# Decode forgetting attention in 32-column tiles of the array, with the cached values whole

## The chip, the core and the metric

One core of a Trainium2 chip runs the whole program in one launch. The metric is device time in microseconds. The kernel before took 3339.79 us (median of three runs, 3335.1 to 3340.51). Its profiled execution took 3333.96 us, of which 3331.8 us lie between the first and the last instruction.

## What is computed

The kernel is one step of a one-layer streaming encoder. A prompt of 2048 tokens and 8 decode streams of 16 new tokens each go through one input projection, three gated branches (forgetting attention, retention, attention into a memory) and an output projection. The change touches the forgetting attention, above all that of the decode streams, where 16 queries of a stream meet 2048 cached tokens and the 16 new ones, for 8 heads of 64:

```python
def fox_attend(q, c_q, q_pos, k, v, c_k):
    s = jnp.einsum('bqhd,bkhd->bhqk', q, k, preferred_element_type=jnp.float32) * (DH_FOX ** -0.5)
    s = s + jnp.swapaxes(c_q, 1, 2)[..., :, None] - jnp.swapaxes(c_k, 1, 2)[..., None, :]
    k_pos = jnp.arange(k.shape[1])
    s = jnp.where(k_pos[None, :] <= q_pos[:, None], s, -jnp.inf)
    p = jax.nn.softmax(s, axis=-1).astype(v.dtype)
    return jnp.einsum('bhqk,bkhd->bqhd', p, v)

# decode: the cache and the new tokens together
k_all = jnp.concatenate([cache_fox_k[l].astype(fk.dtype), fk], axis=1)
v_all = jnp.concatenate([cache_fox_v[l].astype(fv.dtype), fv], axis=1)
c_all = jnp.cumsum(jnp.concatenate([cache_fox_logf[l].astype(jnp.float32), logf], axis=1), axis=1)
fox_o = fox_attend(fq, c_all[:, past:], pos_s, k_all, v_all, c_all)
```

Everything is fp32. Most products are made in the type fp32r, a factor being split into a part that fp32r holds and the rest; some are plain fp32 matmuls.

## The kernel before

After the projection (to about 1690 us) two lanes are woven together by weights. The right lane runs retention and then the prompt's forgetting attention (`fox`: scores at L1290 to L1293, maxima L1297, exponentials L1298, factors by `softmax_scale`, scaling on GpSimd at L1302, transposes L1324, split L202 and L205, values L1344, end L1350 to L1352). The left lane runs a short scan, the prompt's memory attention, the decode memory attention and then `decode_fox`. When `decode_fox` is done the left lane begins the first output block beside the rest of `fox`, and then the other output blocks follow. All stages write their instructions in this woven order, and a scheduler then sets the order on each engine. All loads stand in SyncE's one queue (L184).

`decode_fox` does one `unit` per stream b, 8 of them, a new one entering every 5 steps, so that two or three are alive at once. A unit goes through its keys in four chunks of 512 cached tokens (ci = 0 to 3) and a last one of the 16 new tokens (ci = 4), first for the scores, then for the values.

- Rows of the score: 128 partitions hold 4 pairs of heads, 2 heads of a pair, 16 queries. A key tile `dkt` holds one pair of heads on its 128 partitions. The queries of pair g stand in `qb` as a 128x128 block that is zero but for the 32 columns of that pair (the tile is 160 wide and is read with a stride of 128, so that pair g falls on columns 32g to 32g+31). The four fp32 matmuls of a chunk (L1460) therefore each fill 128 rows, three quarters of them with zeros, and are added up in one bank `ys`; a matmul with 16 rows (L1461) adds the running sum of the forget logarithms from `crow`. `crow` is made at a unit's begin by 16 transposes (L1450) and four copies (L1451).
- L1469 takes the maximum of the chunk, L1471 the exponentials `dpt`. After the last chunk `softmax_scale` makes one factor per chunk: L1221 the smallest of the negated maxima `nmx`, L1222 a subtraction on VectorE, L1223 the exponential on ScalarE. GpSimd scales `dpt` (L1477).
- Values: four transposes (L1487) bring 512 tokens of `dpt` to PSUM, and L202 (ScalarE) and L205 (VectorE) split them into two halves of `dpr`, which stand side by side as 128 columns: 64 of the first part, 64 of the rest. Every 256 cached values `dvt` are split too, L1497 (ScalarE) making `dvh`, and L1499 (GpSimd, twice) the rest `dvl`. Four fp32r matmuls of 256 columns (L1504) for each block of 128 tokens then add into `ov`, tile `ym`. The last chunk uses the new values `dvn`, already split (L1511, L1512). L1514 copies `ov` (128x512), and four matmuls with `sumid` (L1520) add the two halves and transpose.

`softmax_scale` is also called by `fox`, with two blocks of queries (nq = 2).

Of the kernel before, what the change touches and what calls it, by code (L numbers as in the profile page):

```python
# [9 lines left out]
F32 = mybir.dt.float32  # L10
# [62 lines left out]
def body(ctx: ExitStack, tc: tile.TileContext, a, o, stop=99):  # L73
# [106 lines left out]
    def f32(t):  # L180
        return t.bitcast(F32)
# [1033 lines left out]
    def softmax_scale(nmx, l, f, nq, ncx, name):  # L1215

        if ncx == 1:
            V.reciprocal(f, l)
            return None
        nm = sp.tile([P, 2], F32, name=name + "nm")[:, :nq]  # L1220
        V.tensor_reduce(nm, nmx, AX.X, ALU.min)  # L1221
        V.tensor_tensor(f, nm.unsqueeze(2).broadcast_to([P, nq, ncx]), nmx, ALU.subtract)  # L1222
        S.activation(f, f, AF.Exp)  # L1223
        V.scalar_tensor_tensor(l, l, 2.0, f, ALU.mult, ALU.mult)
        V.tensor_reduce(nm, l, AX.X, ALU.add)
        V.reciprocal(nm, nm)  # L1226
        return nm
# [141 lines left out]
    def decode_fox(dp, dw):  # L1369
# [53 lines left out]
        qblk = [dp.tile([P, 4, 160], F32, name=f"qb{i}") for i in range(2)]  # L1423
# [3 lines left out]
        def unit(b):  # L1427

            z = qblk[b % 2]
            for hf in range(2):  # L1430
                rr = slice(64 * hf, 64 * hf + 64)
                G.tensor_copy(z[rr, :, hf * TS:(hf + 1) * TS], qw[rr, :, b * TS:(b + 1) * TS])
            qb = z.rearrange("p g c -> p (g c)")[:, :512].rearrange("p (g c) -> p g c", g=4)
# [18 lines left out]
            for ci in range(5):  # L1452
                sc = pys()
                if ci < 4:
                    w = 512
                    for g2 in range(2):
# [23 lines left out]
            for ci in range(5):  # L1480
# [4 lines left out]
                pr = dw.tile([P, 4, 2, 2, 64], F32R, name="dpr", bufs=1)  # L1485
                for j in range(n):
                    T.transpose(p[:rows, j * P:(j + 1) * P], pts[ci][:, j * P:j * P + rows], ident)  # L1487
                prv = pr.rearrange("p j a r c -> p (j a) r c")[:rows, :2 * n]
                split(prv[:, :, 0], prv[:, :, 1], p[:rows, :n * P].rearrange("p (a c) -> p a c", c=64))
                if ci < 4:  # L1490
                    for j in range(4):
                        if j % 2 == 0:
                            vt = dw.tile([P, 2, 512], F32, name="dvt")
                            dma(vt, vvw[:, 4 * ci + j:4 * ci + j + 2])
                            vh = dw.tile([P, 2, 512], F32R, name="dvh")
                            vl = dw.tile([P, 2, 512], F32R, name="dvl")
                            S.copy(vh, vt)  # L1497
                            for i in range(2):
                                G.tensor_tensor(vl[:, i], vt[:, i], f32(vh)[:, i], ALU.subtract)  # L1499
                        for part in (vh, vl):  # L1500
                            for a2 in range(2):
                                c = slice(a2 * 256, (a2 + 1) * 256)
                                lt = pr[:, j, a2].rearrange("p r c -> p (r c)")
                                T.matmul(ov[:, c], lt, part[:, j % 2, c], start=ci == 0 and j == 0 and a2 == 0 and part is vh, stop=False)  # L1504
                else:
                    vn = dw.tile([16, 8, P], F32R, name="dvn", bufs=1)
                    dma(f32(vn), f32(vhl)[SEQ + b * TS:SEQ + (b + 1) * TS])
                    for a2 in range(2):
                        c = slice(a2 * 256, (a2 + 1) * 256)
                        lt = pr[:16, 0, a2].rearrange("p r c -> p (r c)")  # L1510
                        T.matmul(ov[:, c], lt, vn[:, 4 * a2:4 * a2 + 4, 0:64], start=False, stop=False)  # L1511
                        T.matmul(ov[:, c], lt, vn[:, 4 * a2:4 * a2 + 4, 64:128], start=False, stop=a2 == 1)  # L1512
                    os = dw.tile([P, 512], F32, name="dos", bufs=1)
                    S.copy(os, ov)  # L1514
# [3 lines left out]
            for g4 in range(4):  # L1518
                c0 = 96 * g4 - 32 * (g4 % 2)
                T.matmul(p[:, c0:c0 + 64], os[:, g4 * P:(g4 + 1) * P], sumid, start=True, stop=True)  # L1520
            pv = p[:, :384].rearrange("p (g c) -> p g c", g=4)
# [273 lines left out]
```

## Time and profile before

| | |
|---|---|
| median of three runs | 3339.79 us |
| profiled execution | 3333.96 us |
| its span | 3331.8 us |
| mean granted TensorE clock | 0.978 |
| decode attention beside the prompt's, about 2004 to 2690 us | 686 us |
| TensorE busy in that stretch | 646.75 us |
| ScalarE, VectorE, GpSimd busy in it | 482.11, 480.04, 428.22 us |

TensorE's busy time is the union of its matmuls, and each of them is shown until its last result is out, while the next has begun already. What a matmul costs the engine is therefore read from the distance between two starts, and the `mean ns` of a group is longer than that. A plain fp32 matmul stands in the trace as two records, one behind the other; an fp32r matmul, or a transpose, as one. In the column of shapes, `128*128` is rows and columns of the array in use, and the shape behind it the moving tile. [...]

### The profile page before, as it was taken

To read this page: it belongs to the slowest core of one execution; us is meant where nothing else is said; L and a number is where in the kernel's file an instruction comes from. 1 tells how busy PE (TensorE), PEld (TensorE's weight loads), DVE (VectorE), ACT (ScalarE), POOL (GpSimd) and SP (SyncE) were. 2 spreads that over 40 slices of the span, in tenths; PEclk is the share of its full clock that TensorE was granted. 3 is DMA by queue.
4 is the path that set the end of the run, shared out by engine and by line. 5 is a ranking of instruction groups with operands and counts; after the bars stand their busy time and mean duration, and the time that the engine had idled before them with its cause. 6 is when DMAs were issued, how large, how long until landed. Compare 5 with 4: busy or idle time off the path is not lost.

```text
span 3331.8 us, 57569 instructions
## 1 busy us (share of the span) xinstructions
PE 3164.7 (95%) x21243; PEld 2900.8 (87%) x21243; DVE 2107.7 (63%) x3478; ACT 1655.8 (50%) x3217; POOL 981.8 (29%) x917
## 2 busy tenths in 40 slices
PE   6999999999999999999979978999999999999999
PEld 5999999999999999999969945777777788889899
DVE  7777676756556566556667736766666886554444
ACT  4453444545445455445445635767677774222222
POOL 4446443100210020210011303666665853100100
PEclk8999999999999999999989988999999999999999
DMA  4776565677556658767677875555565458576665
GB/s 165 234 241 210 186 199 192 197 221 238 184 175 202 203 185 244 225 201 212 199 246 236 271 224 174 156 157 163 176 200 156 121 155 252 178 214 198 183 201 160
DMA packets 638445, 660.75 MB, mean 198 GB/s; under 512 B 46060, under 2 KB 553348, under 8 KB 638100
## 3 DMA queue, kind: packets, MB, share of 16 engines
q1 hardware_dynamic: 638164, 657.08, 63.9%
q8 instruction: 168, 2.75, 0.3%
q14 instruction: 113, 0.93, 0.1%
HBM read 477.52 MB, written 179.41 MB: 197 GB/s over the span
## 4 chain that ended last, share of the span: by engine, by line
PE 69%; DMA 11%; DVE 9%; issue 4%; ACT 4%; POOL 2%; SPq 1%; DVEq 0%; ACTq 0%; POOLq 0%
PE a L449 7%; PE a L451 7%; PE a L450 7%; PE b L449 5%; PE b L451 5%; PE b L450 5%; PE ys L1460 3%; PE ov L1344 3%; PE tp L1324 3%; DMA x<-in_x_prompt 2%; DMA out_y_p<-x 2%; DVE wl L400 2%; PE sc L1290 2%; PE ym L1504 2%; PE tp L227 1%
## 5 line engine op out<-in xcount | busy, mean ns | idle before, releaser
L400 DVE TENSOR_TENSOR wl<-wr,wh 128x1024 fp32r<-128x1024 f32 (+1 forms) x386 | 565.1, 1468 | 287.0 <-ACT wh L399 285.1
L399 ACT CAST wh<-wr 128x1024 fp32r<-128x1024 f32 (+1 forms) x386 | 404.6, 1050 | 306.8 <-PE b L451 128.2
L449 PE MATMUL a<-wh,ho 128*128 128x256 f32 (+1 forms) x1432 | 407.3, 285 | 14.7 <-ACT gz L707 8.4
L450 PE MATMUL a<-wl,ho 128*128 128x256 f32 (+1 forms) x1432 | 405.5, 283 | 5.8 <-DVE wl L400 5.8
L451 PE MATMUL a<-wh,ho 128*128 128x256 f32 (+1 forms) x1432 | 406.1, 284 | 0.7 <-DVE ho L276 0.7
L451 PE MATMUL b<-wh,ho 128*128 128x256 f32 (+1 forms) x1032 | 290.8, 282 | 5.4 <-DVE ho L276 5.4
L449 PE MATMUL b<-wh,ho 128*128 128x256 f32 (+1 forms) x1032 | 291.4, 283 | 4.3 <-ACT wh L399 2.3
L450 PE MATMUL b<-wl,ho 128*128 128x256 f32 (+1 forms) x1032 | 290.7, 282 | 0.6 <-DVE wl L400 0.6
L449 PEld LDWEIGHTS a<-wh,ho 128*128 128x128 f32 x1432 | 272.4, 190 | 18.3 <-ACT gz L707 10.4
L221 ACT CAST wh<-wraw 128x1024 fp32r<-128x1024 f32 x120 | 122.9, 1049 | 331.0 <-DMA wraw<-in_w_p 121.7
L428 POOL TENSOR_TENSOR wr<-wr 128x1024 f32<-128x1024 f32 (+1 forms) x72 | 200.1, 2779 | 272.1 <-DMA wr<-in_w_in 219.7
L450 PEld LDWEIGHTS a<-wl,ho 128*128 128x128 f32 x1432 | 272.6, 190 | 6.3 <-DVE wl L400 6.3
L451 PEld LDWEIGHTS a<-wh,ho 128*128 128x128 f32 x1432 | 272.6, 190 | 1.3 <-DVE ho L276 1.3
L449 PE MATMUL a<-ho,wh 128*128 128x384 f32 (+1 forms) x768 | 253.0, 329 | 1.8 <-ACT gz L707 1.7
L450 PE MATMUL a<-ho,wh 128*128 128x384 f32 (+1 forms) x768 | 253.3, 330 | 0.0
L451 PE MATMUL a<-ho,wl 128*128 128x384 f32 (+1 forms) x768 | 252.6, 330 | 0.0
L460 ACT COPY kp<-a 128x256 f32<-128x256 f32 (+3 forms) x384 | 152.9, 404 | 183.3 <-PE a L451 182.7
L1297 DVE TENSOR_REDUCE f_mx<-sc 128x1 f32<-128x512 f32 (+2 forms) x320 | 192.2, 604 | 66.1 <-PE sc L1293 33.1
L1302 POOL TENSOR_SCALAR pt<-pt,f_f,f_nm 128x512 f32<-128x512 f32 (+3 forms) x288 | 206.0, 730 | 93.8 <-DVE f_nm L1226 78.7
L1298 ACT ACTIVATE pt<-sc,f_mx 128x512 f32<-128x512 f32 (+2 forms) x320 | 200.8, 628 | 63.5 <-DVE f_mx L1297 55.7
L205 DVE TENSOR_TENSOR pl<-tp,ph 128x512 fp32r<-128x512 f32 (+2 forms) x352 | 193.0, 562 | 55.8 <-ACT ph L202 52.9
L451 PEld LDWEIGHTS b<-wh,ho 128*128 128x128 f32 x1032 | 195.1, 189 | 5.6 <-DVE ho L276 5.6
(375 smaller groups left out, 8819.0 us busy)
## 6 DMA issues: line engine op xcount, KB each, us to landing
wr<-in_w_in SPq DMA_DIRECT2D x170, 512.0 KB
wraw<-in_w_p SPq DMA_DIRECT2D x80, 512.0 KB
dkt<-in_cache_fox_k SPq DMA_DIRECT2D x64, 512.0 KB
dvt<-in_cache_fox_v SPq DMA_DIRECT2D x64, 512.0 KB
wr<-sum_gl SPq DMA_DIRECT2D x48, 512.0 KB
wraw<-in_w_out SPq DMA_DIRECT2D x40, 512.0 KB
gtd<-gz SPq DMA_DIRECT2D x96, 192.0 KB
gt<-gtd SPq DMA_DIRECT2D x24, 768.0 KB
```

What stands on the lines that cost most here:

```text
L205: V.tensor_tensor(l, src, f32(h), ALU.subtract)
L221: S.copy(whv[:, i * hc:(i + 1) * hc], rv)
L399: S.copy(h, t)
L400: eng.tensor_tensor(l, t, f32(h), ALU.subtract)
L428: G.tensor_tensor(out, x, y, op)
L449: T.matmul(out, lh(c), rh(c), start=first and c == 0, stop=False, skip_group_check=True)
L450: T.matmul(out, lh(c), rl(c), start=False, stop=False, skip_group_check=True)
L451: T.matmul(out, ll(c), rh(c), start=False, stop=last and c == 3, skip_group_check=True)
L460: S.copy(t[nm], t["a"])
L1297: V.tensor_reduce(nmx[:, j, ci:ci + 1], sc[:, :w], AX.X, ALU.max, negate=True)
L1298: S.activation(pt[:, :w], sc[:, :w], AF.Exp, bias=nmx[:, j, ci:ci + 1], accum_out=l[:, j, ci:ci + 1])
L1302: G.tensor_scalar(pt, pt, fb, 0.5 if r is None else r[:, j:j + 1], ALU.mult, ALU.mult)
```

## The change

Four things are changed, all of them in `decode_fox` but the last.

- Scores. `qb` is 32 columns wide for each pair, without zeros for the other pairs. The matmul of a pair writes the 32 partitions of its own rows only, so it takes a tile of 128 rows by 32 columns of the array, and the four pairs take four different tiles. The matmul with `crow` (or `cnT`, and the mask) over all 128 rows comes first now and opens the bank; before, it came last.
- Values. The probabilities are copied whole (`dpr` 128x512, ScalarE, no rest by VectorE), and the cached values are not split. Each block of 128 tokens has four fp32 matmuls, one for each pair, with 32 columns of the array and 128 moving columns, again in four tiles. The new values are added up from their two parts by VectorE (`dvw`) and multiplied in tiles of 32 columns too. `dvt` has 4 buffers (2 before), `dpr` 2 (1 before).
- End of a unit. `ov` is 128x128 and holds every pair's own rows, so one transpose takes the place of four matmuls.
- `softmax_scale`: the subtraction on VectorE goes; ScalarE makes exp(nm - nmx) at once, with scale and bias, one instruction for each block of queries (two in `fox`, one in `decode_fox`).

```diff
@@ softmax_scale
-        V.tensor_tensor(f, nm.unsqueeze(2).broadcast_to([P, nq, ncx]), nmx, ALU.subtract)
-        S.activation(f, f, AF.Exp)
+        for q in range(nq):
+            S.activation(f[:, q], nmx[:, q], AF.Exp, scale=-1.0, bias=nm[:, q:q + 1])
@@ decode_fox
-        qblk = [dp.tile([P, 4, 160], F32, name=f"qb{i}") for i in range(2)]
+        qblk = [dp.tile([P, 4, 32], F32, name=f"qb{i}") for i in range(2)]
@@ unit, scores
                     for g2 in range(2):
                         kt = dw.tile([P, 2, 512], F32, name="dkt", bufs=4)
                         dma(kt, kv[:, 2 * g2:2 * g2 + 2, ci * 512:(ci + 1) * 512])
-                        for g in range(2):
-                            T.matmul(sc, qb[:, 2 * g2 + g], kt[:, g], start=g2 == 0 and g == 0, stop=False)
-                    T.matmul(sc, selr[32 * ci:32 * ci + 16], crow[32 * ci:32 * ci + 16], start=False, stop=True)
+                        kts += [kt[:, 0], kt[:, 1]]
+                    T.matmul(sc, selr[32 * ci:32 * ci + 16], crow[32 * ci:32 * ci + 16], start=True, stop=False)
+
+                    for g4 in range(4):
+                        T.matmul(sc[32 * g4:32 * g4 + 32], qb[:, g4], kts[g4], start=False, stop=True)
@@ last chunk
-                    for g4 in range(4):
-                        T.matmul(sc[:, :16], qb[:, g4], kw[:, g4, bs], start=g4 == 0, stop=False)
-                    T.matmul(sc[:, :16], selr[:16], cnT[:, bs], start=False, stop=False)
-                    T.matmul(sc[:, :16], identb, dmask, start=False, stop=True)
+                    T.matmul(sc[:, :16], selr[:16], cnT[:, bs], start=True, stop=False)
+                    T.matmul(sc[:, :16], identb, dmask, start=False, stop=False)
+                    for g4 in range(4):
+                        T.matmul(sc[32 * g4:32 * g4 + 32, :16], qb[:, g4], kw[:, g4, bs], start=False, stop=True)
@@ values
-                split(prv[:, :, 0], prv[:, :, 1], p[:rows, :n * P].rearrange("p (a c) -> p a c", c=64))
+                S.copy(pr[:rows, :n], p[:rows, :n * P].rearrange("p (j c) -> p j c", c=P))
...
-                            vh = dw.tile([P, 2, 512], F32R, name="dvh")
-                            vl = dw.tile([P, 2, 512], F32R, name="dvl")
-                            S.copy(vh, vt)
-                            for i in range(2):
-                                G.tensor_tensor(vl[:, i], vt[:, i], f32(vh)[:, i], ALU.subtract)
-                        for part in (vh, vl):
-                            for a2 in range(2):
-                                c = slice(a2 * 256, (a2 + 1) * 256)
-                                lt = pr[:, j, a2].rearrange("p r c -> p (r c)")
-                                T.matmul(ov[:, c], lt, part[:, j % 2, c], start=ci == 0 and j == 0 and a2 == 0 and part is vh, stop=False)
+                        for g4 in range(4):
+                            g = slice(32 * g4, 32 * g4 + 32)
+                            T.matmul(ov[g, :P], pr[:, j, g], vt[:, j % 2, g4 * P:(g4 + 1) * P], start=ci == 0 and j == 0, stop=False)
@@ end of a unit
-                T.matmul(p[:, c0:c0 + 64], os[:, g4 * P:(g4 + 1) * P], sumid, start=True, stop=True)
+            T.transpose(p[:, :P], os, ident)
```

The order of instructions changes with it. On TensorE, at the third chunk of the second stream's scores (near 2115 us in the trace), this stood before; `ys` is the bank of the scores, `ym` that of the values, and the other rows are the prompt's attention:

```order
L1324 MATMUL tp<-kc,pt 128x128 x4
L1460 MATMUL ys<-dkt,qb_22193 128x512 x4
L1461 MATMUL ys<-crow,selr 128x512
L1290 MATMUL sc<-ka,qa 128x128
L1291 MATMUL sc<-kb,qb 128x128
L1293 LDWEIGHTS identb
L1293 MATMUL sc<-maskb,identb 128x128
L1504 MATMUL ym<-dvh,dpr 128x256 x2
L1504 MATMUL ym<-dvl,dpr 128x256 x2
```

and this stands there now (line numbers are those of the changed kernel: L1460 is the matmul with `crow`, L1463 the four pairs' scores, L1499 the values):

```order
L1324 MATMUL tp<-kc,pt 128x128 x4
L1499 MATMUL ym<-dvt,dpr 32x128 x12
L1344 MATMUL ov<-pl,vv 128x128
L1499 MATMUL ym<-dvt,dpr 32x128 x4
L1324 MATMUL tp<-kc,pt 128x128 x7
L1460 MATMUL ys<-crow,selr 128x512
L1463 MATMUL ys<-dkt,qb_22193 32x512 x4
L1290 MATMUL sc<-ka,qa 128x256
L1291 MATMUL sc<-kb,qb 128x256
```

The four matmuls of a chunk still stand together behind each other, with `crow`'s ahead of them; a chunk's 16 value matmuls stand in one or two runs. In the whole changed program the value matmuls of cached tokens stand in 42 runs and the score matmuls in 36.

On TensorE at the first chunk of the first stream, where the running sums are not made yet, this stood before (L1396 is the first matmul of what makes those sums):

```order
L1291 MATMUL sc<-kb,qb 128x512
L1460 MATMUL ys<-dkt,qb_22192 128x512 x4
L1290 MATMUL sc<-ka,qa 128x512
L1291 MATMUL sc<-kb,qb 128x512
L1290 MATMUL sc<-ka,qa 128x384
L1291 MATMUL sc<-kb,qb 128x384
L1293 LDWEIGHTS identb
L1293 MATMUL sc<-maskb,identb 128x128
L1396 MATMUL tp<-ctot,sufm 128x64
```

and now:

```order
L1396 MATMUL tp<-ctot,sufm 128x64
L1401 MATMUL tp<-lfs,kc 128x8
L1408 MATMUL tp<-identr,cnr 16x128
L1419 MATMUL tp<-kc,lq 128x1
L1449 MATMUL tp<-identr,cb 16x128 x8
L1419 MATMUL tp<-kc,lq 128x1
L1449 MATMUL tp<-identr,cb 16x128 x4
L1460 MATMUL ys<-crow,selr 128x512
L1463 MATMUL ys<-dkt,qb_22192 32x512 x4
```

The scores of that first chunk moved behind the making of the sums and behind `crow`.

On ScalarE, in the second stream, this stood before (`pt` are the prompt's exponentials, `dpt` the decode streams'):

```order
L1451 CAST crow<-tp 16x512
L1298 ACTIVATE pt,f_l<-sc,f_mx 128x384
L1497 CAST dvh<-dvt 128x1024
L1298 ACTIVATE pt,f_l<-sc,f_mx 128x512
L1223 ACTIVATE f_f<-f_f 128x2x2
L1497 CAST dvh<-dvt 128x1024
L1451 CAST crow<-tp 16x512 x3
L1350 COPY f_ot<-ov 64x256
L1471 ACTIVATE dpt,d_l<-ys,d_mx 128x512
```

and this stands there now (L1450, L1473 and L1223 are the same steps as L1451, L1471 and L1223 before):

```order
L1350 COPY f_ot<-ov 64x256
L1298 ACTIVATE pt,f_l<-sc,f_mx 128x384
L1450 CAST crow<-tp 16x512
L1298 ACTIVATE pt,f_l<-sc,f_mx 128x512
L1223 ACTIVATE f_f<-f_mx,f_nm 128x2 x2
L1450 CAST crow<-tp 16x512 x2
L1350 COPY f_ot<-ov 64x256
L1450 CAST crow<-tp 16x512
L1298 ACTIVATE pt,f_l<-sc,f_mx 128x512
```

The two casts of 128x1024 that stood between the prompt's exponentials are gone, and the factors' exponential is two instructions where it was one.

## Rows read from the trace of the kernel before

**Rows 1.** The profile's page: busy time, share of the span and instructions of each engine.

```profile
PE 3164.7 (95%) x21243; PEld 2900.8 (87%) x21243; DVE 2107.7 (63%) x3478; ACT 1655.8 (50%) x3217; POOL 981.8 (29%) x917
```

**Rows 2.** Busy time by stretch: the stretch and its length, then busy us (instructions) of PE, PEld, DVE, ACT and POOL, the granted clock, the share of the DMA engines and GB/s.

```profile
2100.00:2600.00 500.00, 481.61 (x2960) 373.96 (x2959) 339.25 (x773) 357.18 (x907) 327.41 (x400) 0.98 0.57 170
...
2690.00:2780.00 90.00, 83.08 (x645) 78.21 (x644) 75.93 (x122) 52.25 (x107) 53.71 (x47) 0.99 0.60 172
2004.00:2690.00 686.00, 646.75 (x3958) 503.70 (x3958) 480.04 (x1113) 482.11 (x1233) 428.22 (x531) 0.96 0.55 162
```

**Rows 3.** The chain that ended last within 2100 to 2690 us, by line.

```profile
by line: PE ys L1460 15.9%; PE ov L1344 14.8%; PE tp L1324 13.0%; PE ym L1504 8.9%; PE sc L1290 7.6%; PE sc L1291 6.3%; issue 4.3%; ACT pt L1298 3.2%; DVE f_mx L1297 2.9%; PE tp L1487 2.1%; DVE pl L205 1.9%; PE ys L1461 1.9%; DMA qb<-qtH 1.
```

**Rows 4.** TensorE's waits within 2010 to 2690 us: who waited for whom, us in total, times, the longest.

```profile
PE sc L1290 <- ACT pt L1298: 16.2, 28, 2.8
PE ym L1504 <- DVE dpr L205: 3.7, 4, 1.5
...
PE sc L1290 <- ACT dvh L1497: 2.4, 1, 2.4
```

**Rows 5.** TensorE in order of time: start, us to the last end, line, rows*columns of the array, moving shape, count of merged records.

```profile
2115.52 3.60 PE L1460 MATMUL ys<-dkt,qb 128*128 128x512 f32 x8
2119.05 0.50 PE L1461 MATMUL ys<-crow,selr 16*128 16x512 f32 x1
2119.48 0.33 PE L1290 MATMUL sc<-ka,qa 128*128 128x128 f32 x1
...
2120.11 0.40 PE L1504 MATMUL ym<-dvl,dpr 128*128 128x256 f32 x2
2120.35 0.40 PE L1504 MATMUL ym<-dvh,dpr 128*128 128x256 f32 x2
2120.59 0.40 PE L1504 MATMUL ym<-dvl,dpr 128*128 128x256 f32 x2
```

**Rows 6.** The same view a little earlier: the prompt's scores right behind a matmul with `crow`, and the transposes of a decode chunk.

```profile
2112.37 0.50 PE L1290 MATMUL sc<-ka,qa 128*128 128x512 f32 x1
2112.71 0.40 PE L1291 MATMUL sc<-kb,qb 68*128 68x512 f32 x1
2112.94 0.40 PE L1344 MATMUL ov<-ph,vv 128*128 128x256 f32 x2
...
2113.53 0.60 PE L1487 MATMUL tp<-kc,dpt 128*128 128x128 f32 x4
```

**Rows 7.** The same view at the end of a score chunk of the first stream.

```profile
2042.16 0.49 PE L1461 MATMUL ys<-crow,selr 16*128 16x512 f32 x1
2042.16 0.38 PE L1419 MATMUL tp<-kc,lq 16*128 16x1 f32 x2
2042.58 0.50 PE L1344 MATMUL ov<-ph,vv 128*128 128x256 f32 x2
```

**Rows 8.** The same view: the matmuls of the new tokens' scores, and those with `sumid`.

```profile
2060.36 1.07 PE L1466 MATMUL ys<-dkw,qb 128*128 128x16 f32 x8
...
2174.43 1.00 PE L1520 MATMUL tp<-sumid,dos 128*128 128x64 f32 x8
```

**Rows 9.** The same view where `crow`'s transposes run, which use 16 columns of the array.

```profile
2100.21 0.40 PE L1344 MATMUL ov<-pl,vv 128*128 128x256 f32 x2
2100.44 0.40 PE L1450 MATMUL tp<-identr,cb 128*16 128x128 f32 x4
2100.68 0.44 PE L1290 MATMUL sc<-ka,qa 128*128 128x512 f32 x1
2100.96 0.40 PE L1291 MATMUL sc<-kb,qb 68*128 68x512 f32 x1
```

**Rows 10.** The same view: the first chunk of the first stream, the matmul behind it, and the first matmul with `crow`.

```profile
2016.50 5.30 PE L1460 MATMUL ys<-dkt,qb 128*128 128x512 f32 x8 [0.81 <-POOL qb L1432]
2021.23 0.79 PE L1290 MATMUL sc<-ka,qa 128*128 128x512 f32 x1
...
2033.30 0.79 PE L1461 MATMUL ys<-crow,selr 16*128 16x512 f32 x1
```

**Rows 11.** Groups of instructions within 2000 to 2690 us, shapes kept apart: names, shapes, count, busy us, mean ns of one, idle time before them and who ended it.

```profile
L1499 POOL TENSOR_TENSOR dvl<-dvt,dvh 128x512 fp32r<-128x512 f32 x128 | 160.5, 1279 | 76.9 <-PE ym L1504 43.8 <-ACT dvh L1497 27.3 <-PE ov L1344 2.8
...
L1460 PE MATMUL ys<-dkt,qb 128*128 128x512 f32 x256 | 119.6, 610 | 1.6 <-ACT dpt L1471 0.8 <-POOL qb L1432 0.8
...
L1497 ACT CAST dvh<-dvt 128x1024 fp32r<-128x1024 f32 x64 | 66.5, 1045 | 23.4 <-DMA dvt<-in_cache_fox_v 10.4 <-PE ym L1504 6.2 <-issue 5.4
...
L1504 PE MATMUL ym<-dvh,dpr 128*128 128x256 f32 x256 | 54.0, 293 | 3.8 <-DVE dpr L205 3.7
L1504 PE MATMUL ym<-dvl,dpr 128*128 128x256 f32 x256 | 52.9, 288 | 0.0
...
L205 DVE TENSOR_TENSOR dpr<-tp,dpr 128x512 fp32r<-128x512 f32 x32 | 21.9, 684 | 6.1 <-ACT dpr L202 6.1
...
L1222 DVE TENSOR_TENSOR f_f<-f_nm,f_mx 128x4 f32<-128x4 f32 x15 | 10.0, 665 | 0.6
...
L1223 ACT ACTIVATE f_f<-f_f 128x4 f32<-128x4 f32 x16 | 3.3, 206 | 4.2 <-DVE f_f L1222 4.1
```

**Rows 12.** SyncE's queue, the waits for GpSimd's split of the cached values within 2010 to 2690 us.

```profile
SPq L184 <- POOL dvl L1499: 45.0, 29, 6.5
```

More of the change, by code (lines that the diff above doesn't have):

```diff
@@ L1427, in unit @@
         def unit(b):
-            z = qblk[b % 2]
+            qb = qblk[b % 2]
             for hf in range(2):
                 rr = slice(64 * hf, 64 * hf + 64)
-                G.tensor_copy(z[rr, :, hf * TS:(hf + 1) * TS], qw[rr, :, b * TS:(b + 1) * TS])
-            qb = z.rearrange("p g c -> p (g c)")[:, :512].rearrange("p (g c) -> p g c", g=4)
+                G.tensor_copy(qb[rr, :, hf * TS:(hf + 1) * TS], qw[rr, :, b * TS:(b + 1) * TS])
             cs = dw.tile([P, 16, 8], F32, name="cs")
@@ L1455, in unit @@
                     w = 512
+                    kts = []
                     for g2 in range(2):
@@ L1483, in unit @@
                 rows = P if ci < 4 else 16
-                pr = dw.tile([P, 4, 2, 2, 64], F32R, name="dpr", bufs=1)
+                pr = dw.tile([P, 4, P], F32, name="dpr")
                 for j in range(n):
                     T.transpose(p[:rows, j * P:(j + 1) * P], pts[ci][:, j * P:j * P + rows], ident)
-                prv = pr.rearrange("p j a r c -> p (j a) r c")[:rows, :2 * n]
-                split(prv[:, :, 0], prv[:, :, 1], p[:rows, :n * P].rearrange("p (a c) -> p a c", c=64))
+                S.copy(pr[:rows, :n], p[:rows, :n * P].rearrange("p (j c) -> p j c", c=P))
                 if ci < 4:
@@ L1492, in unit @@
                         if j % 2 == 0:
-                            vt = dw.tile([P, 2, 512], F32, name="dvt")
+                            vt = dw.tile([P, 2, 512], F32, name="dvt", bufs=4)
                             dma(vt, vvw[:, 4 * ci + j:4 * ci + j + 2])
-                            vh = dw.tile([P, 2, 512], F32R, name="dvh")
-                            vl = dw.tile([P, 2, 512], F32R, name="dvl")
-                            S.copy(vh, vt)
-                            for i in range(2):
-                                G.tensor_tensor(vl[:, i], vt[:, i], f32(vh)[:, i], ALU.subtract)
-                        for part in (vh, vl):
-                            for a2 in range(2):
-                                c = slice(a2 * 256, (a2 + 1) * 256)
-                                lt = pr[:, j, a2].rearrange("p r c -> p (r c)")
-                                T.matmul(ov[:, c], lt, part[:, j % 2, c], start=ci == 0 and j == 0 and a2 == 0 and part is vh, stop=False)
+                        for g4 in range(4):
+                            g = slice(32 * g4, 32 * g4 + 32)
+                            T.matmul(ov[g, :P], pr[:, j, g], vt[:, j % 2, g4 * P:(g4 + 1) * P], start=ci == 0 and j == 0, stop=False)
                 else:
@@ L1507, in unit @@
                     dma(f32(vn), f32(vhl)[SEQ + b * TS:SEQ + (b + 1) * TS])
[L1508 to L1514, printed above, removed]
+                    vw = dw.tile([16, 8, 64], F32, name="dvw", bufs=1)
+                    V.tensor_tensor(vw, f32(vn)[:, :, 0:64], f32(vn)[:, :, 64:128], ALU.add)
+                    for g4 in range(4):
+                        g = slice(32 * g4, 32 * g4 + 32)
+                        T.matmul(ov[g, :P], pr[:16, 0, g], vw[:, 2 * g4:2 * g4 + 2].rearrange("p h d -> p (h d)"), start=False, stop=True)
+                    os = dw.tile([P, P], F32, name="dos", bufs=1)
+                    S.copy(os, ov[:, :P])
                 yield
             p = pdt()
-            for g4 in range(4):
-                c0 = 96 * g4 - 32 * (g4 % 2)
-                T.matmul(p[:, c0:c0 + 64], os[:, g4 * P:(g4 + 1) * P], sumid, start=True, stop=True)
-            pv = p[:, :384].rearrange("p (g c) -> p g c", g=4)
+            T.transpose(p[:, :P], os, ident)
+            pv = p[:, :P].rearrange("p (g c) -> p g c", g=4)
             bs = slice(b * TS, (b + 1) * TS)
```

## The prediction

> **What bounds the kernel now.** The page comes first: TensorE is busy for 95% of the span, the next engine for 63% [rows 1]. Then the stretch in which the decode attention runs beside the prompt's: of 686 us TensorE is busy 646.75, ScalarE 482.11, VectorE 480.04, GpSimd 428.22, at a clock of 0.96 [rows 2]. The chain that ended last within it is made of TensorE's lines; its largest entry, 15.9%, is the decode scores' L1460, and the decode values' L1504 has 8.9% [rows 3]. TensorE waits little there: 16.2 us for the prompt's exponentials, 3.7 for the split probabilities, 2.4 for the cast `dvh` [rows 4]. So the stretch lasts as long as TensorE's instructions do, and the question is what the new matmuls cost that engine. ScalarE, VectorE and GpSimd matter by a few of its waits only.
>
> Busy time is no price, since matmuls overlap in their tails. I use distances between starts. L1460's eight records take (3.60 - 0.59)/7 = 0.43 us each, 0.59 being the last one's own length; so one fp32 matmul of 512 columns, two records, costs 0.86 us. L1504's pairs start 0.24 us apart, 0.12 for one fp32r matmul of 256 columns [rows 5]. L1291, fp32r of 512 columns, has 0.23; a transpose of 128 fp32 columns has (0.60 - 0.27)/3 = 0.11 [rows 6]. A record of plain fp32 therefore takes twice as long for a column as fp32r, and 0.11 us is what I take for a record of 128 columns.
>
> **Scores.** Now 32 chunks with 8 records each: 256 x 0.43 = 110.1 us. The changed kernel has the same 256 records of 512 columns. What they cost depends on one thing that this trace doesn't show: whether matmuls in different column tiles run at the same time. If they run one after another, the price stays 110.1. If all four run together, a chunk takes two records' time, 0.86, and 32 of them 27.5 us. For some overlap there is a near row: at 2042.16 the matmul with `crow` (16 rows of the array from partition 32 on) and the first record of L1419 (16 rows from partition 0 on) start at the same hundredth, where another matmul behind `crow` starts 0.43 later [rows 5, 7]. So tiles of rows do run together. Against four at once speak the two records of a matmul: they need the same tile, stand behind each other, and nothing in the trace overtakes. The second record of pair 0 waits for the first; pair 1's first can then start beside it. That gives five steps for eight records: 5 x 0.43 = 2.15 us for a chunk, 68.8 in all, **41.3 us less**. It also asks for only two fp32 streams at once, and that rate the moving side delivers to L1291 already (0.23 against 0.43). I take this.
>
> **Values.** Now 512 x 0.12 = 61.4 us. Changed: 128 blocks x 4 pairs = 512 fp32 matmuls of 128 columns, 1024 records of 0.11. One after another 112.6 us; in pairs, as above, one step for each matmul and one more for each of the 42 runs, 554 x 0.11 = 60.9; four at once 28.2. I take 60.9: **0.5 less**. What is saved here is on other engines: 64 casts `dvh` of 1045 ns on ScalarE, 128 subtractions `dvl` of 1279 ns on GpSimd, 32 of 684 ns on VectorE [rows 11].
>
> **End of a unit and new tokens.** The 64 records with `sumid` cost (1.00 - 0.27)/7 = 0.104 each, 6.7 us, and 8 transposes of 0.11 follow: 5.8 less. The 64 records of L1466 have (1.07 - 0.25)/7 = 0.117, though only 16 columns move: they go at the pace of loading 128 columns of weights. With 32 columns of weights the nearest row is L1450's, 16 columns, four starts in 0.24, 0.06 each [rows 8, 9]: 3.7 less. The 32 fp32r matmuls of the new values (0.12) become 64 records that run in pairs: 1 us more at most.
>
> **Change of tiles.** The matmul with `crow` costs more than its columns: L1460's last record, at 2115.52 + 7 x 0.43, starts 0.52 before it and not 0.43, it holds the engine 0.43 and not 0.23, and the next L1290 0.34 and not 0.23 [rows 5, 6]. Into another shape of tile and back is some 0.38 us. The other shape in the trace is L1450's 16 columns: it starts on time, and the L1290 behind it takes 0.28 instead of 0.23, so 0.05 for both ways [rows 9]. The change adds one step for each of the 36 score runs (rows, then columns, then whole), both ways for 42 value runs, and about 9 pairs in the last chunks: some 69 ways there and back, 3.5 us by the one row and 26 by the other. I take 14, near the middle: columns are what L1450 uses, but its fp32r transposes aren't the same form.
>
> [...]
>
> **The first chunk.** It is moved. Before, stream 0's first four score matmuls ran from 2016.50 to 2021.23, in a hole in which TensorE had little else, 17 us ahead of the first `crow` matmul at 2033.30 [rows 10]. Now they stand behind that. The sum above counts this chunk as 1.29 saved; in truth its 2.15 us come on top: 3.4 more.
>
> **Waits.** `dpr` needs one copy by ScalarE instead of a copy and a subtraction by VectorE, and no cast `dvh` stands between the prompt's exponentials: of the 22 us of waits [rows 4] I take 6 away; the ends are 0 and 20. `dvt` gets two more buffers, and SyncE's queue, which stood 45.0 us behind `dvl` with the prompt's loads behind it [rows 12], is blocked less; I count nothing for it, since TensorE hardly waits for loads. In `softmax_scale` VectorE loses some 50 subtractions (665 ns in the commonest group) and ScalarE gets one exponential of 206 ns more for each unit of the prompt [rows 11], some 10 us against the 66.5 it is rid of. Nothing on TensorE waited for either, so this costs nothing; were ScalarE the bound, it would still be a gain. The crow-first order makes the four matmuls wait for `crow`, and TensorE's queue behind them; from the second stream on it is made long before.
>
> **Sum.** -41.3 - 0.5 - 5.8 - 3.7 + 1 + 14 + 3.4 - 6 = **-39 us**. The profiled execution would go from 3334 to 3295. The median of the runs lies 5.8 above that execution; I predict 3339.8 - 39 = **3301**.
>
> **Rivals.**
> - *Column tiles take turns.* Rows of different tiles have their own partitions; column tiles all read the same 128 partitions, so that L1419's overlap with `crow` needn't carry over. Then scores save nothing, values cost 51.2 us more, and the rest is -5.8 - 3.7 + 3 + 14 + 3.4 - 6 = +5: +56, **3396**. It decides from here: the records' serial 222.7 us (110.1 + 112.6) shrink by a factor f and stand against 171.5 now; with the 5 us of the other terms f has to exceed 1.34 for a gain, and two at a time give 1.7. Against it speak the overlap in [rows 7] and the rate of two streams.
> - *All four at once.* Each tile has its own line, and a matmul's second record doesn't hold up the next pair. Scores save 82.6, values 33.2; with the rest -114. The stretch would then be some 570 us with ScalarE at about 420, VectorE 440, so more of the prompt's waits show; I give 15 back: -99, **3241**. [...]
> - *The gain is taken by something else.* With TensorE eased, the prompt's chain of maxima, exponentials and transposes sets the pace. For it: the 16.2 us behind the exponentials. Against it: after 2690 us, without decode attention, TensorE is still 83.08 of 90 busy [rows 2]. Then the kernel stays within 7 us: **3337**.
>
> **Chances.** Two at a time 0.47, four at once 0.25, taking turns 0.18, gain taken elsewhere 0.10. The range reaches from the four-at-once case with less lost to other engines, 3230, to the last rival's end, 3342; it leaves out the case of turns and little else. A measurement of this kernel can tell about 0.2%, 7 us, from no change. Faster by more than that: both overlap cases but for a little of the first, 0.70; slower: the turns and a little, 0.20; the same: 0.10.
>
> **What would show it.** Between starts of the score records in one chunk: 0.43 throughout means turns; starts in pairs, five steps in 2.15 us, the forecast; four starts within some hundredths, four at once. Value runs of 16 matmuls should take 1.9 us against 1.9 before. `dvh` and `dvl` must be gone, GpSimd near 270 us in the stretch, and the matmul behind a tile run should start 0 to 0.2 us late. [...]

## The result and the profile after

The changed kernel takes 3237.62 us (median of four runs, 3236.31 to 3242.14), the kernel before 3337.74 in the four runs beside it: a ratio of 0.9698 (95% interval 0.9686 to 0.9711), 100 us less where 39 were forecast. The profiled execution fell from 3333.96 to 3236.31 us, its span from 3331.8 to 3234.5.

The page of the kernel after, as in [rows 1]:

```profile
PE 3061.6 (95%) x21731; PEld 2813.4 (87%) x21731; DVE 2034.8 (63%) x3390; ACT 1605.4 (50%) x3201; POOL 826.4 (26%) x789
```

TensorE is still busy for 95% of the span. Its busy time fell by 103 us, the span by 97. GpSimd lost 155 us, ScalarE 50, VectorE 73.

Busy time by stretch, columns as in [rows 2]; the stretch of both attentions now ends near 2590 us, and the one behind it starts there:

```profile
2590.00:2680.00 90.00, 84.39 (x652) 79.64 (x653) 71.58 (x126) 55.10 (x116) 58.33 (x51) 0.98 0.57 164
2004.00:2590.00 586.00, 541.92 (x4444) 415.12 (x4444) 417.25 (x1025) 428.64 (x1208) 269.30 (x400) 0.94 0.63 189
```

It is 100 us shorter, and that is the whole gain. TensorE is without work for 44 of 586 us there, against 39 of 686 before. The granted clock is 0.94 against 0.96, and ScalarE is busy for 73% of it, against 70%.

The chain that ended last within 2100 to 2590 us, by line, and TensorE's waits within 2010 to 2590 us, as in [rows 3, 4]:

```profile
by line: PE ov L1344 17.7%; PE tp L1324 15.3%; PE sc L1290 9.1%; PE sc L1291 7.3%; PE ym L1499 6.4%; DMA dkt<-in_cache_fox_k 6.2%; PE ys L1463 5.1%; ACT pt L1298 4.7%; issue 3.3%; DVE f_mx L1297 3.0%; PE tp L1489 2.1%; DMA qa<-qtL 1.9%; DVE
```

```profile
PE sc L1290 <- ACT pt L1298: 18.0, 31, 2.0
```

The decode scores, now L1463, went from 15.9% of the chain to 5.1%. The prompt's lines lead it. TensorE's wait for the prompt's exponentials is about as long as before, 18.0 us against 16.2, in a shorter stretch.

TensorE in order of time: the scores of a chunk behind `crow`'s matmul, those of the new tokens, and a run of values; columns as in [rows 5]:

```profile
2101.98 0.50 PE L1460 MATMUL ys<-crow,selr 16*128 16x512 f32 x1
2102.40 1.07 PE L1463 MATMUL ys<-dkt,qb 128*32 128x512 f32 x8
2103.40 0.39 PE L1290 MATMUL sc<-ka,qa 128*128 128x256 f32 x1
...
2115.62 0.26 PE L1470 MATMUL ys<-dkw,qb 128*32 128x16 f32 x8
2115.81 0.66 PE L1324 MATMUL tp<-kc,pt 128*128 128x128 f32 x4
...
2251.85 1.08 PE L1499 MATMUL ym<-dvt,dpr 128*32 128x128 f32 x32
2252.86 0.66 PE L1324 MATMUL tp<-kc,pt 128*128 128x128 f32 x4
```

These rows are the result. Eight score records hold the engine for 1.00 us, from 2102.40 to 2103.40; in [rows 5] eight took 3.53. Two records, one behind the other, are 0.86, so the eight take two steps and 0.14 for the way back to whole matmuls: all four tiles run at once. Record by record, four start within 0.02 us and the other four 0.45 behind them. In the trace 28 chunks stand in one run each. The other four are cut in two halves of two pairs, and a half takes as long as a whole chunk:

```profile
2161.44 1.05 PE L1463 MATMUL ys<-dkt,qb 128*32 128x512 f32 x4
2162.43 0.33 PE L1290 MATMUL sc<-ka,qa 128*128 128x128 f32 x1
```

That makes 36 score runs of about 1.00 us, but for two at a granted clock of 0.50 (1.87 us) and two that wait for keys in their middle. Thirty-two value records hold it for 1.01 us, 0.032 each where 0.11 was the price of one by itself.

The tiles' own view (all of L1463 and of L1499: count, shortest, median and longest ns, first and last start):

```profile
L1463 PE MATMUL ys<-dkt,qb x256: 592/617/1062, 2032.2 to 2495.8; 128*32 128x512 f32 x128
```

```profile
L1499 PE MATMUL ym<-dvt,dpr x1024: 272/273/423, 2089.0 to 2568.4; 128*32 128x128 f32 x171
```

### The profile page after: what moved, and what is told of

It is laid out like the page before. It is cut to its first block, busy times and chain, and to the rows that moved or that the text cites. A ratio compares the mean times of both kernels' runs of the same rounds, so it can differ in the third digit from the quotient of the medians.

```text
span 3234.5 us, 58278 instructions
## 1 busy us (share of the span) xinstructions
PE 3061.6 (95%) x21731; PEld 2813.4 (87%) x21731; DVE 2034.8 (63%) x3390; ACT 1605.4 (50%) x3201; POOL 826.4 (26%) x789
## 4 chain that ended last, share of the span: by engine, by line
PE 70%; DMA 12%; DVE 8%; ACT 3%; issue 3%; POOL 2%; SPq 1%; DVEq 0%; ACTq 0%; POOLq 0%
PE a L449 7%; PE a L451 7%; PE a L450 7%; PE b L449 5%; PE b L451 5%; PE b L450 5%; PE ov L1344 3%; PE tp L1324 3%; PE sc L1290 2%; DMA out_y_p<-x 2%; DVE wl L400 2%; DMA x<-in_x_prompt 2%; PE tp L226 1%; PE tp L227 1%; PE tp L228 1%
```

## The experiments

The theory (theory 1) was: all four tiles run at once, and the time that TensorE saves is the gain. The rival: the relief of the other engines, which no longer split the probabilities and cached values, gave it. Later runs test two parts of these, with names of their own. "Above" in what follows is how far a run lies above the changed kernel: (its ratio - 0.9698) x 3337.74. The intervals make that uncertain by some 6 to 11 us.

**Scores as before.** The changed kernel with whole score matmuls of 128 columns, `crow` last; the values stay in tiles.

```diff
-                    for g4 in range(4):
-                        T.matmul(sc[32 * g4:32 * g4 + 32], qb[:, g4], kts[g4], start=False, stop=True)
+                        for g in range(2):
+                            T.matmul(sc, qb[:, 2 * g2 + g], kt[:, g], start=g2 == 0 and g == 0, stop=False)
```

> The changed kernel with the scores alone as before (four matmuls over the whole array with zero-padded queries, the matmul with crow last). Theory 1, column tiles run at the same time and TensorE sets the pace: the scores' records go from about 27 us back to 110, so 70 to 83 us more than the changed kernel, 3307 to 3321 us. Rival, the gain came from ScalarE, GpSimd and VectorE being rid of the splits, which this kernel keeps: under 10 us more, 3238 to 3248 us.

Measured: 3289.34 us, ratio 0.9837 [0.9815, 0.9859], 46 above. TensorE is the bound again, and shows it:

```profile
2004.00:2590.00 586.00, 561.03 (x3961) 415.92 (x3960) 378.60 (x921) 383.72 (x1074) 241.21 (x362) 0.95 0.59 177
```

The matmuls count, but for less than theory 1 said. The old scores hold TensorE some 77 us longer (32 chunks of 3.53 against 36 runs of 1.00); 46 of them show in the medians, 59 in the profiled execution, which took 3295.39 us. Part of the rest is filled in: TensorE stands without work for 25 of 586 us here and for 44 in the changed kernel.

**Values as before.** Splits, whole matmuls and the end of a unit of the kernel before; the scores stay in tiles.

```diff
+                            S.copy(vh, vt)
+                            for i in range(2):
+                                G.tensor_tensor(vl[:, i], vt[:, i], f32(vh)[:, i], ALU.subtract)
...
-                            T.matmul(ov[g, :P], pr[:, j, g], vt[:, j % 2, g4 * P:(g4 + 1) * P], start=ci == 0 and j == 0, stop=False)
+                                T.matmul(ov[:, c], lt, part[:, j % 2, c], start=ci == 0 and j == 0 and a2 == 0 and part is vh, stop=False)
```

> The changed kernel with the values and the end of a unit as before (split probabilities and cached values, fp32r over the whole array, the four matmuls with sumid). Theory 1: 33 us more for the values' matmuls, 6 for those with sumid and up to 15 for waits behind the casts, 3270 to 3292 us. Rival: the splits are back on ScalarE, GpSimd and VectorE, and most of the 100 us with them, 3310 us or more.

Measured: 3280.57 us, ratio 0.9818 [0.9786, 0.985], 40 above. This agrees with theory 1, but doesn't tell the matmuls from the splits.

**The splits kept.** The changed kernel, with the rest of the probabilities on VectorE and the casts and subtractions of cached values made as before and read by nobody.

```diff
+                    V.tensor_tensor(prl, p, pr.rearrange("p j c -> p (j c)"), ALU.subtract)
...
+                            S.copy(vh, vt)
+                            for i in range(2):
+                                G.tensor_tensor(vl[:, i], vt[:, i], f32(vh)[:, i], ALU.subtract)
```

> The changed kernel with the splits of the cached values and of the probabilities still made by ScalarE, GpSimd and VectorE as before, their results read by nobody. TensorE's matmuls are those of the changed kernel. Theory 1: these engines have room, 0 to 15 us more than the changed kernel, 3237 to 3253 us. Rival: the relief of these engines was the gain, 3300 us or more.

Measured: 3289.47 us, ratio 0.9843 [0.982, 0.9866], 48 above. Neither fits: TensorE has every one of its fast matmuls, and half the gain is gone. The stretch shows where:

```profile
2004.00:2590.00 586.00, 506.59 (x4029) 382.19 (x4027) 420.20 (x956) 438.29 (x1147) 394.88 (x485) 0.92 0.59 179
```

TensorE is without work for 79 of 586 us, and no engine is busy for more than 87% of it. Theory 1 by itself fell here. What VectorE's part costs alone was not tried.

**One engine's split at a time.** First ScalarE's 64 casts alone, then GpSimd's 128 subtractions alone (of the cached values from themselves); both are read by nobody.

```diff
+                            vh = dw.tile([P, 2, 512], F32R, name="dvh")
+                            S.copy(vh, vt)
```

```diff
+                                G.tensor_tensor(vl[:, i], vt[:, i], vt[:, i], ALU.subtract)
```

> The changed kernel with ScalarE's cast of the cached values kept (64 of 1.05 us, read by nobody). Theory A, these casts stand between the prompt's exponentials in ScalarE's queue and were what the kept splits cost: 30 to 50 us more than the changed kernel. Theory B, GpSimd's subtractions were: under 12 us more.

> The changed kernel with two subtractions of 128x512 on GpSimd kept for every 256 cached values (128 in all, reading the cached values alone, since no cast is there to subtract; read by nobody). Theory A, ScalarE's casts were what the kept splits cost: under 12 us more than the changed kernel. Theory B, GpSimd's 160 us delay the scaling of the prompt's probabilities and the loads behind them: 30 to 50 us more.

Measured: ScalarE's 3278.93 us, ratio 0.9821 [0.9804, 0.9838], 41 above; GpSimd's 3250.63 us, ratio 0.9733 [0.9718, 0.9749], 12 above. So it is ScalarE's casts for the larger part. Their own view says how long ScalarE stood before them:

```profile
L1498 ACT CAST dvh<-dvt x64: 1032/1047/1091, 2024.8 to 2585.5; 128x1024 fp32r<-128x1024 f32 x64
its engine sat idle before it (us, times) until:
  DMA dvt<-in_cache_fox_v: 41.5, 31
```

and ScalarE in order of time shows one such place, TensorE the answer to it:

```profile
2183.12 0.57 ACT L202 CAST ph<-tp 128x512 fp32r<-128x512 f32 x1
2184.73 1.05 ACT L1498 CAST dvh<-dvt 128x1024 fp32r<-128x1024 f32 x1 [1.03 <-DMA dvt<-in_cache_fox_v]
2185.68 0.68 ACT L1298 ACTIVATE pt<-sc,f_mx 128x512 f32<-128x512 f32 x1
```

```profile
2185.32 0.40 PE L1344 MATMUL ov<-pl,vv 128*128 128x256 f32 x2
2186.50 0.50 PE L1290 MATMUL sc<-ka,qa 128*128 128x512 f32 x1 [0.79 <-ACT pt L1298]
```

The cast waits for a load; the prompt's exponentials are next on the same engine, and TensorE's next scores wait for those. Over 2010 to 2590 us these waits grew: TensorE waited 18.0 us for the exponentials in the changed kernel and nothing of note for L202; with the casts kept it waited

```profile
PE sc L1290 <- ACT pt L1298: 29.9, 45, 2.2
PE ov L1344 <- ACT ph L202: 9.9, 6, 5.4
```

and 51 us for ScalarE in all, against 19. A third way, that the casts hold the buffers of cached values longer and so put off the loads, doesn't show: SyncE's queue has no wait for a cast `dvh` in this trace. Two mechanisms were left: the waits for loads (A1), or the casts' own 67 us ahead of the exponentials (A2).

**The same casts without a load to wait for.** A first try cast a tile that never changes.

```diff
+        res = dp.tile([P, 2, 512], F32, name="dres")
+        V.memset(res, 0.0)
...
+                            S.copy(vh, res)
```

> The changed kernel with 64 casts of 128x1024 on ScalarE at the places where the cached values were cast, but of a tile that lies in SBUF all the time, so that they take ScalarE's 67 us and wait for no load. Theory A1, in the kernel that kept the cast ScalarE's queue stood behind casts that waited for their load (41.5 us in its trace): most of its 41 us go, 0 to 18 us more than the changed kernel, 3238 to 3256 us. Theory A2, ScalarE's own time was what it cost: 30 to 45 us more.

Measured: 3270.86 us, ratio 0.9791 [0.977, 0.9811], 31 above. It tells nothing: with nothing to wait for, all 64 casts were put at the start of the stretch.

```profile
L1500 ACT CAST dvh<-dres x64: 1027/1050/1179, 2013.8 to 2121.2; 128x1024 fp32r<-128x1024 f32 x64
```

In the next pair one run ties the casts to the chunk's probabilities, which ScalarE itself has just written, and the other has the casts of cached values again, with 7 buffers `dvt` in place of 4.

```diff
+                            S.copy(vh, pr.rearrange("p j c -> p (j c)").unsqueeze(1).broadcast_to([P, 2, 512]))
```

```diff
-                            vt = dw.tile([P, 2, 512], F32, name="dvt", bufs=4)
+                            vt = dw.tile([P, 2, 512], F32, name="dvt", bufs=7)
...
+                            S.copy(vh, vt)
```

> After, with 64 casts of 128x1024 put on ScalarE in the decode, two in a chunk, at the places of the kept casts of cached values, but reading the chunk's transposed probabilities, which ScalarE itself has just written; the results are read by nobody. ScalarE's time grows by 64 x 1.05 = 67 us, as with the kept casts of cached values, but none of these casts can wait for a load. Theory A1 (the kept casts cost 41 us because ScalarE's queue stood before loads of cached values that had not landed, 41.5 us in that trace): at most 18 us above the changed kernel, 3238 to 3256. Theory A2 (the prompt's exponentials are late because of ScalarE's own time in front of them): 30 to 45 us above, 3268 to 3283, with ScalarE idle before no such cast.

> After, with ScalarE's 64 casts of the cached values kept (read by nobody), as in the run that cost 41 us, and seven buffers of cached values in place of four, so that a load is asked for up to three buffers earlier. Theory A1 (the waits for loads cost the time): ScalarE's 41.5 us of idle time before these casts fall below 15, and the time falls to within 20 us of the changed kernel, 3240 to 3258. Theory A2 (ScalarE's own time): the waits may fall, the time stays 30 to 45 us above it, 3268 to 3283.

Measured: tied casts 3247.35 us, ratio 0.9721 [0.9706, 0.9736], 8 above; seven buffers 3284.51 us, ratio 0.9826 [0.9805, 0.9848], 43 above. The tied casts run spread over the stretch and take as long:

```profile
L1498 ACT CAST dvh<-dpr x64: 1027/1048/1092, 2098.2 to 2579.4; 128x1024 fp32r<-128x1024 f32 x64
```

TensorE's waits for ScalarE grow less, to 25 us in all over 2010 to 2590 us:

```profile
PE sc L1290 <- ACT pt L1298: 21.9, 40, 1.8
PE ov L1344 <- ACT ph L202: 1.0, 1, 1.0
```

So 67 us more of ScalarE's time cost 8, and as many casts behind loads 41, which speaks for A1. The two runs differ in one thing more: the tied casts can't begin before the chunk's probabilities are there, so they also stand at other places in ScalarE's order (from 2098.2 us on, the others from 2024.8). In the run with seven buffers the waits hardly fell, so it did not do what A1 had foreseen, and tells the two apart no further:

```profile
  DMA dvt<-in_cache_fox_v: 35.0, 29
```

**Factors.** The changed kernel with VectorE's subtraction back; and the new factors alone in the kernel before.

```diff
-        for q in range(nq):
-            S.activation(f[:, q], nmx[:, q], AF.Exp, scale=-1.0, bias=nm[:, q:q + 1])
+        V.tensor_tensor(f, nm.unsqueeze(2).broadcast_to([P, nq, ncx]), nmx, ALU.subtract)
+        S.activation(f, f, AF.Exp)
```

> The changed kernel with the softmax's chunk factors as before, a subtraction on VectorE and one exponential on ScalarE. Theory 1: nothing on TensorE waits for them, within 5 us of the changed kernel, 3232 to 3243 us. Rival: the shorter way from maxima to factors lets the prompt's attention run ahead and is part of the gain, 8 to 20 us more.

> The kernel before with the new chunk factors alone (ScalarE alone, no subtraction). As my prediction had it, TensorE sets the pace there and nothing on it waits for the factors: within 5 us of the kernel before, whose median is near 3341 us here. Rival, they save the 10 to 14 us that the changed kernel loses without them in any kernel: 3327 to 3331 us.

Measured: 3251.93 us, ratio 0.9729 [0.9714, 0.9743], 10 above; alone 3340.66 us, ratio 0.9999 [0.9987, 1.0011]. The same edit is worth nothing where TensorE hides it and some 10 us where it is eased.

**How the tiles run.** Four runs change the tiles of the changed kernel: each score matmul in two parts of 128 and 384 columns; the values' four blocks of one pair in a row, pair after pair; score tiles of 64 columns, two pairs to a tile; and `crow`'s matmul with all 128 rows, those of the other chunks zero in a wider selector.

```diff
-                        T.matmul(sc[32 * g4:32 * g4 + 32], qb[:, g4], kts[g4], start=False, stop=True)
+                        T.matmul(sc[32 * g4:32 * g4 + 32, :128], qb[:, g4], kts[g4][:, :128], start=False, stop=False)
+                        T.matmul(sc[32 * g4:32 * g4 + 32, 128:], qb[:, g4], kts[g4][:, 128:], start=False, stop=True)
```

```diff
-                        for g4 in range(4):
-                            g = slice(32 * g4, 32 * g4 + 32)
+                    for g4 in range(4):
+                        g = slice(32 * g4, 32 * g4 + 32)
+                        for j in range(4):
```

```diff
-                        T.matmul(sc[32 * g4:32 * g4 + 32], qb[:, g4], kts[g4], start=False, stop=True)
+                        T.matmul(sc[64 * (g4 // 2):64 * (g4 // 2) + 64], qb[:, g4], kts[g4], start=False, stop=g4 % 2 == 1)
```

```diff
-                    T.matmul(sc, selr[32 * ci:32 * ci + 16], crow[32 * ci:32 * ci + 16], start=True, stop=False)
+                    T.matmul(sc, sel4[:, ci], crow, start=True, stop=False)
```

> The changed kernel with each pair's score matmul cut into one of 128 moving columns and one of 384, both in the pair's tile, standing behind each other. The two shapes tell in the trace who starts first. Theory 1: the 128-column records of all four pairs start ahead of pair 0's 384-column ones, a chunk takes about 0.9 to 1.0 us, the kernel within 10 us of the changed one. Rival, starts in the order of the program: pair 0 has all four records done before pair 1 has its second, some 2.8 us for a chunk, 45 to 60 us more.

> The changed kernel with a chunk's 16 value matmuls in another order: all four blocks of tokens for the first tile, then all four for the second, and so on, so that 8 records of one tile stand behind each other. Theory 1, a record that waits for its own tile doesn't hold up those of other tiles behind it: a chunk still takes about 1.1 us, within 8 us of the changed kernel. Rival, starts in the order of the program: tiles overlap only where one tile's run meets the next, about 2.9 us for a chunk, 45 to 60 us more.

> The changed kernel with the scores in tiles of 64 columns: two pairs share a tile, half of whose weights are zeros. Two tiles at a time, 8 records of 0.43 us in two lines: 1.72 us for a chunk instead of 0.87, 27 us more of TensorE in 32 chunks. Theory 1: 15 to 27 us more than the changed kernel, 3253 to 3265 us. Rival, the number of tiles doesn't matter as long as TensorE is not the only bound: under 6 us more.

> The changed kernel with crow's matmul over all 128 rows of the array (the rows of the other chunks meet weights of zero), so that the array goes from whole to columns and back and never to 16 rows for a cached chunk. If each change of tiles costs 0.1 to 0.2 us of TensorE, 32 chunks save 3 to 12 us, 3225 to 3235 us. Rival, waits take it: within 3 us of the changed kernel.

Measured: two parts 3245.69 us, ratio 0.9721 [0.9696, 0.9745], 8 above; pair after pair 3268.47, ratio 0.9787 [0.9773, 0.9802], 30 above; 64 columns 3252.49, ratio 0.9731 [0.9709, 0.9753], 11 above; `crow` whole 3239.31, ratio 0.9692 [0.9668, 0.9716], not to be told from the changed kernel. Two parts came out as theory 1 had it and `crow` whole as its rival; the other two lie between their two forecasts.

The first two were made to see whether a record may start ahead of one that waits for its own tile. With two parts, TensorE's instructions stand in the compiled program as part and part of one pair, then those of the next (`32x128` is stationary columns by moving columns; each stands for two records, and the brackets name semaphores that it waits for):

```
L1460 MATMUL ys<-crow,selr 128x512
L1463 MATMUL ys<-dkt,qb_22192 32x128 [waits DMAHW6_49,Pool_49]
L1464 MATMUL ys<-dkt,qb_22192 32x384
L1463 MATMUL ys<-dkt,qb_22192 32x128
L1464 MATMUL ys<-dkt,qb_22192 32x384
```

TensorE in order of time in that run:

```profile
2158.70 0.49 PE L1460 MATMUL ys<-crow,selr 16*128 16x512 f32 x1
2159.11 0.45 PE L1463 MATMUL ys<-dkt,qb 128*32 128x128 f32 x8
2159.36 0.85 PE L1464 MATMUL ys<-dkt,qb 128*32 128x384 f32 x8
2160.14 0.55 PE L1324 MATMUL tp<-kc,pt 128*128 128x128 f32 x3
```

All eight records of 128 columns have started before the first of 384 does, 0.25 us behind the first of them, though pair 0's 384 stand ahead of the others' 128. Waiting records are passed: the last pair's are ahead of six that precede them in the program, two of each other pair. The values pair after pair show a limit:

```profile
2156.56 2.46 PE L1501 MATMUL ym<-dvt,dpr 128*32 128x128 f32 x32
2158.95 0.65 PE L1449 MATMUL tp<-identr,cb 128*16 128x128 f32 x8
```

The 32 value records take 2.39 us here, eight in a row for each tile, against 1.01 in the changed kernel where the tiles alternate. With all tiles at work it would be eight steps, the same as there. As an estimate, 2.39 less the 0.17 that a value run takes beyond its steps in the changed kernel are some 20 steps of 0.11: eight for the first tile and four more for each other one. A tile's first record would then start beside the fifth of the tile before it, so that three waiting ones of that tile are passed, and not seven. The 64-column tiles give 1.88 for a chunk, two at a time:

```profile
2111.48 1.95 PE L1465 MATMUL ys<-dkt,qb 128*64 128x512 f32 x8
2113.36 0.55 PE L1324 MATMUL tp<-kc,pt 128*128 128x128 f32 x3
```

against 1.00, so 32 x 0.88 = 28 us more on TensorE, of which 11 show.

## Why the prediction was off

The direction and the bound were right: TensorE set the stretch's length, and its instructions became cheaper. GpSimd's busy time in the stretch, forecast near 270 us, is 269.30; the matmul behind a run of tiles comes 0.14 to 0.17 late, within the 0 to 0.2 that were named. The size was wrong by more than half, at these steps.

**Scores, the step that failed.** The prediction said that a matmul's two records "stand behind each other, and nothing in the trace overtakes", and made five steps of a chunk's eight records, 41.3 us less. In the trace after they take two: 36 runs of 1.00 where 32 chunks of 3.53 stood, 77 less. The run in two parts shows why: a record that waits for its tile doesn't hold up the next tile's (eight records of 128 columns start within 0.25 us, ahead of the first of 384). That nothing overtook in the trace of before was no evidence, since almost nothing there used another tile.

**Values, the same step.** Forecast 0.5 less, by pairs; measured 32 x 1.01 = 32 us where 61.4 had been, 29 less.

**Change of tiles.** Forecast 14. A chunk has 1.00 - 0.86 = 0.14, a value run 1.01 less 32 x (1.08 - 0.27)/31 = 0.84, so 0.17; for 32 and 42 of them about 12. It is in the two numbers above already, so the term was sized well.

**New tokens, end of a unit, first chunk.** The new tokens' eight records hold TensorE for 0.19 us a unit (2115.62 to 2115.81) against 0.94, 6.0 less where 3.7 were taken. Their weight loads, 32 columns each, take 0.16 for all eight (L1470); those of 128 columns took 0.97 in the kernel before (L1466). The end of a unit isn't measured apart. The first score now starts at 2032.2, behind the hole, as the step on the first chunk said.

**Sum on TensorE.** -77 - 29 - 6, with the prediction's own -5.8 for the end of a unit and +3.4 for the first chunk: about -114, and the profiled execution shows -98. Sixteen come back: about 5 as more time without work (44 us against 39), and some 12 with the clock, an estimate that sets the 586 us at 0.94 against 0.96.

**Waits and the other engines, the term that was mis-sized.** It took 6 us off, with 0 and 20 as ends, and gave the relief of the other engines nothing else. In the trace after, the wait for the exponentials isn't shorter. Yet without that relief 48 of the 100 us would have been lost. The 22 us of waits were read at the pace of a busier TensorE. With it eased and the casts kept, ScalarE's queue stands 41.5 us before loads (10.4 before, [rows 11]) while the prompt's exponentials are behind, and TensorE waits 51 us for ScalarE, against 19 without the casts. That the kernel before had more work on TensorE to cover such a wait fits these numbers, but was not tested for the casts. The factors are the same case in small: "costs nothing" held in the kernel before, where they bring nothing either, and 10 us hang on them in the changed one. Through which wait these 10 go was not tested.

**The rivals.** Four at once, 3241, came within 4 us, and its mechanism is the one that the trace shows. That the number is so close is in part luck: it took 82.6 and 33.2 less for scores and values, where 77 and 29 were measured, and gave 15 back for waits, where the time without work grew by 5. That tiles take turns was excluded by the first chunk in the trace. That the gain is taken by something else was half right as a mechanism: some half of the gain would have gone that way had the splits stayed.

The parts don't add up to shares of the gain: scores undone cost 46, values undone 40, the splits alone 48, more than the 100 us together.

## What to carry to other kernels

Four matmuls that fill a quarter of the array's columns each were put in four column tiles here and cost little more than one, 1.00 us against 0.86; write them so that the tiles alternate, since eight records in a row for one tile held up the others (2.39 us against 1.01 for 32 records). When the busiest engine is eased, look next at what stands before a load in the queue of the engine that feeds it (41.5 us on ScalarE with its casts kept): work that TensorE hid before may then cost much of the gain, here some 40 of 100 us. Undo the parts one at a time before crediting any of them.

## What the runs showed of the hardware

Records of different column tiles start out of program order. In the run in two parts eight records of 128 columns start within 0.25 us, and the 384 columns that precede six of them in the program start behind, so that the last pair's pass two waiting ones of each other tile. In the value run pair after pair, 2.39 us for 32 records fit three passed ones of a tile and no fourth, by the estimate above. Only starts are compared here.

A group of VectorE's subtractions for the factors (L1222, 128x4) took 665 ns in the kernel before [rows 11] and 196 in the changed kernel with the old factors, with the same shape. The trace of the kernel before shows beside what it was stretched. There the six of the 15 beside which GpSimd ran nothing took 153 to 165 ns. Of the nine beside a GpSimd instruction, eight took 259 to 2084 ns, and six of these eight ended 19 to 24 ns behind the end of a GpSimd instruction; the four longest stood beside `dvl`'s subtractions (L1499), which the change removed. The changed kernel with the old factors has no such subtractions:

```profile
L1222 DVE TENSOR_TENSOR f_f<-f_nm,f_mx 128x4 f32<-128x4 f32 x16 | 3.1, 196 | 0.6
```
